# Up projection of a gated MLP: the high weights against both halves of the activations in one product

## The chip, the cores and the metric

The kernel runs on one core of a Trainium2 chip. The time is that of one execution on the device, in microseconds; of several executions the median is given. TensorE (PE) multiplies, with its weight loads (PEld) shown apart; VectorE (DVE), ScalarE (ACT) and GpSimd (POOL) do the elementwise work; SyncE (SP) issues the transfers from device memory. PSUM is the memory that TensorE writes its sums to. A bank of it holds 512 columns of 32-bit numbers on 128 partitions.

## The reference, cut to what matters

One decoder layer over 256 tokens with 2048 channels: a token mixer and then a channel mixer, both normalised and modulated by a vector. The change is in the channel mixer:

```python
def conv_ffn(h, w_up, conv_w, conv_b, w_down):
    a, g = jnp.split(h @ w_up, 2, axis=-1)
    a = causal_dwconv(a, conv_w, conv_b)
    return (jax.nn.silu(a) * g) @ w_down
```

Here `h` is 256 x 2048, `w_up` 2048 x 11264 (5632 columns for `a`, 5632 for the gate `g`), the convolution runs over 3 tokens, and `w_down` is 5632 x 2048. All of it is in 32-bit floats.

## The kernel before, in words

**Three products for one.** TensorE multiplies in a rounded 32-bit format (`F32R`). To keep the accuracy, each operand is split into a high part, rounded to that format, and a low part, the rest: `w = wh + wl`, `x = xh + xl`. The product is taken as `wh xh + wh xl + wl xh`; the last term, low times low, is left out. `load_split` (lines 141 to 168) does this for weights: a transfer of a chunk of 128 x 1024 into `w` (line 124, a ring of seven buffers), a cast on ScalarE into `wh` (line 147) and a subtraction on VectorE into `wl` (line 150). `wh` and `wl` have four buffers each (`WB = (7, 4, 4)`, line 42). The activations are split once, when they are made: `h2T` holds, for each of 16 row blocks k, the high half `h2T[:, k, 0]` and the low half `h2T[:, k, 1]`, 256 tokens each, side by side.

**The up projection.** `up(j)` (lines 1533 to 1566) makes one block j of 128 columns of `a` and the 128 columns of the gate that belong to it; there are 44 blocks. It takes one bank, `ps_up`: the first 256 columns for `a`, the other 256 for the gate. The weights of a side (b = 0 for `a`, 1 for the gate) come in two chunks (hf) of eight row blocks each. For each row block `mm_b` issues three products with the weights as the stationary operand (128 x 128) and the 256 tokens as the moving one. The moving operand is read through `turns`, which alternates between token b and token 128 + b, so the columns of the bank are in that order as well. Blocks 0 and 1 are done otherwise: their product was made before, row-wise, together with the second normalisation, and `up` only transposes it.

After the products `up` does the rest of the block on ScalarE and VectorE: the convolution (an activation with scale and bias at line 1554, four multiply-adds at lines 1558 and 1560), silu (line 1562), the multiplication by the gate (line 1563), and the split of the result into `uTt`, high (line 1565) and low (line 1566). These read `a` and `gate`, two halves of the bank, straight from PSUM.

**The order of the work.** `up` runs for j = 2, 0, 1, 3 ... 21, then the down projection of this half (`proj_rows`, 512 columns to a product, `ps_d`), then `up` for j = 22 ... 43, then the down projection of the second half. In the first half a `Ticker` also feeds in the modulation of the last residual: at `tk.tick(UR)` after each chunk, with `UR = 0.5`, every second chunk brings one transfer of `w_ada` and one multiply-and-sum over 128 x 1024 on VectorE (line 263). The order on each engine in these stretches is made by a planner, which simulates the engines; each engine then works its list off in order and waits by semaphores. Loads are issued on SP's queue in the order of their chunks, as soon as a buffer of the ring is free. Only the second normalisation before and the last normalisation after have their order written out by hand.

**Buffers.** The pool `psm` has four banks, taken in turn by `ps_up`, `ps_d` and others. Small tiles (`t2`) share eight buffers, taken in turn as well; `av`, the working tile of a block, is one of them.

Of the kernel before, what the change touches and what calls it, by code (L numbers as in the profile page):

```python
# [14 lines left out]
P = 128  # L15
S = 256
# [64 lines left out]
def build(ctx: ExitStack, tc: tile.TileContext, d, out, dbg=None):  # L81
    nc = tc.nc
# [8 lines left out]
    psm = ctx.enter_context(tc.tile_pool(name="psm", bufs=4, space=PSUM))  # L91
# [10 lines left out]
    xt = p0.tile([P, 2, D], F32, name="xt", tag="t16")  # L102
# [5 lines left out]
    def mm(o, lhsT, rhs, start, stop):  # L108
        nc.tensor.matmul(o, lhsT, rhs, start=start, stop=stop)  # L109

    def turns(ap):

        return ap.rearrange("p (a b) -> p b a", a=2)

    def t2(shape, name, dt=F32):
        return p0.tile(shape, dt, name=name, tag="t2", bufs=NT2)

    def bank(pool, name, dt=F32):
        return pool.tile([P, 512], dt, name=name, tag="b")
# [21 lines left out]
    def load_split(src, off=0, t=None, after=None, n0=None):  # L141

        n = src.shape[-1]
        if t is None:
            t = load(src)
        wh, wl = halves(off)
        hi = nc.scalar.copy(wh[:, :n], t[:, :n])  # L147
        while moved:
            behind(moved.pop(0)(), hi)
        lows.append(nc.vector.tensor_sub(wl[:, :n], t[:, :n], wh[:, :n]))  # L150
        if after:
            behind(lows[-1], after)
        while added and n0 not in AHEAD[7]:
            behind(lows[-1], added.pop())
        pairs[n0] = hi, lows[-1]
        while slow:
            behind(slow.pop(), lows[-1])
        for nth, ns in AHEAD.items():
            if n0 in ns and nth in wides:
                behind(wides[nth], lows[-1])  # L160
        if n0 == AHEADMOD and blocks:
            behind(blocks[0], hi)
        if fresh:
            fresh[1] -= 1
            if fresh[1] < 0:
                behind(hi, fresh[0])
                fresh.clear()
        return wh, wl
# [5 lines left out]
    def mm_b(ps, wh, wl, i, xt, k, start, stop):  # L174
        a, b = wh[:, i * P:(i + 1) * P], wl[:, i * P:(i + 1) * P]
        xh, xl = [turns(xt[:, k, x, :]) for x in range(2)]
        mm(ps, a, xh, start, False)
        mm(ps, a, xl, False, False)
        mm(ps, b, xh, False, stop)

    def mm_a(ps, xt, k, t, wh, wl, start, stop):
        xh, xl = xt[:, k, 0, t * P:(t + 1) * P], xt[:, k, 1, t * P:(t + 1) * P]
        wh, wl = turns(wh), turns(wl)
        mm(ps, xh, wh, start, False)
        mm(ps, xh, wl, False, False)
        mm(ps, xl, wh, False, stop)
# [33 lines left out]
    for i in range(4):  # L220
        ps = bank(psm, "ps_c")
# [132 lines left out]
    def big(name, offset=0):  # L354

        t = p0.tile([P, 2 * KD * S + OFFN], F32R, name=name, tag="hT")[:, offset:offset + 2 * KD * S]
        return t.rearrange("p (k a b) -> p k a b", k=KD, a=2)
# [111 lines left out]
    with tc.manual_schedule(engines={mybir.EngineType.DVE, mybir.EngineType.Activation, mybir.EngineType.PE}):  # L469
# [5 lines left out]
        sums = [next(second) for _ in range(2)]  # L475
# [290 lines left out]
    for gi, kn in enumerate(GROUPS):  # L766
# [24 lines left out]
        for b, ks in order_b(gi):  # L791
# [3 lines left out]
            ps = psb[j]  # L795
            whole = j < HELD
            shared = j < HELD + 4
            for k in ks:
                need(k0 + k)
                wh, wl = next(wb)  # L800
                o = ps[:, (b % 2) * S:(b % 2 + 1) * S]
                opening = k == 0 and (not shared or b % 2 == 0 and (not whole or gi == 0))
                new = first.setdefault(k, tiles[0]) == tiles[0]
                if tiles[0] <= 5:
                    continue
                end = k == kn - 1 and (not shared or b % 2 == 1 and not (whole and nxt))
                if not new:
                    catch_up()
                    mm_b(o, wh, wl, 0, hT, k0 + k, opening, end)
                else:  # L810
                    mm(o, wh, turns(hT[:, k0 + k, 0, :]), opening, False)
                    mm(o, wl, turns(hT[:, k0 + k, 0, :]), False, False)
                    lag.append((o, wh, turns(hT[:, k0 + k, 1, :]), False, end))
# [19 lines left out]
        for c in range(6):  # L833
            pss = [bank(psm, "ps_a%d" % t) for t in range(2)]
            aw = AW if c < 4 else 512
            for k in range(k0, k0 + kn):
                need(k)
                wh, wl = next(wa if c < 4 else wv)
# [484 lines left out]
    h2T = big("h2T")  # L1323
# [209 lines left out]
    def up(j):  # L1533

        if j < 2:
            ps = bank(psm, "ps_up")
            for t in range(2):
                for b in range(2):
                    c = (2 * b + j) * P
                    nc.tensor.transpose(ps[:, b * S:(b + 1) * S].rearrange("p (k t) -> p t k", t=2)[:, t],  # L1540
                                        ub[t][:, c:c + P], ident)
        else:
            ps = bank(psm, "ps_up")
            for b in range(2):
                for hf in range(2):
                    wh, wl = load_split(d["w_up"][j * 4 + b * 2 + hf], OFFB[hf])
                    for k in range(8):
                        mm_b(ps[:, b * S:(b + 1) * S], wh, wl, k, h2T, hf * 8 + k, hf == 0 and k == 0,
                             hf == 1 and k == 7)
                    tk.tick(UR)  # L1550
        a, gate = ps[:, :S], ps[:, S:]
        fw = lambda i: ffn[:, 3 * j + i:3 * j + i + 1]
        av = t2([P, S], "av")
        nc.scalar.activation(av, a, AF.Identity, bias=ffn[:, R_FB + j:R_FB + j + 1], scale=fw(2))
        aa, vv = [x.rearrange("p (k t) -> p t k", t=2) for x in (a, av)]
        for i in (1, 0):
            sh = 2 - i
            nc.vector.scalar_tensor_tensor(av[:, 2 * sh:], a[:, :S - 2 * sh], fw(i), av[:, 2 * sh:],
                                           op0=ALU.mult, op1=ALU.add)
            nc.vector.scalar_tensor_tensor(vv[:, 1, :sh], aa[:, 0, P - sh:], fw(i), vv[:, 1, :sh],  # L1560
                                           op0=ALU.mult, op1=ALU.add)
        nc.scalar.activation(av, av, AF.Silu)
        nc.vector.tensor_mul(av, av, gate)
        hi, lo = [uTt[:, j % KH, x, :].rearrange("p (t k) -> p t k", t=2) for x in range(2)]
        nc.scalar.copy(hi, vv)
        nc.vector.tensor_sub(lo, vv, hi)
# [4 lines left out]
    for j in (2, 0, 1, *range(3, KH)):  # L1571
        up(j)
        if j == 2:
            for c in range(2):
                tk.add(ada_rows(5, g2, c))
# [3 lines left out]
    for j in range(KH, KF):  # L1579
        up(j)  # L1580
# [189 lines left out]
```

## Time and profile before

| | |
|---|---|
| median of 3 runs | 1386.07 us (1385.78 to 1386.64) |
| the profiled execution | 1386.17 us, its span 1384.2 us |
| TensorE busy | 1364.6 us, 9234 products |
| VectorE busy | 1059.6 us |
| ScalarE busy | 705.6 us |
| granted TensorE clock | 1.0 |
| first half of the up projection | 690 to 908 us of the span |
| first down projection | 909 to 1023 us |
| second half of the up projection | 1023 to 1259 us |
| second down projection and the last normalisation | 1259 to 1384 us |

A row of a group of instructions names line, engine, operation, output <- inputs, shapes, count; then the busy time in us and the mean ns of one; then the idle time of the engine just before them and what ended it. Products overlap in the engine, so the mean duration of one is longer than the time from start to start. Most products have line 109, the helper `mm`, and are told apart by their output tile. In the chain of waits a row gives start, length and what was at work; in a view by stretches, the busy time of each engine in that stretch.

### The profile page before, as it was taken

What the parts mean: (1) busy time and instruction counts of PE and PEld (TensorE: products, weight loads), DVE (VectorE), ACT (ScalarE), POOL (GpSimd) and SP (SyncE); (2) the same over time, 40 slices, a digit from 0 to 9 for tenths busy, and PEclk for the clock granted to TensorE, in tenths of its full rate; (3) what the DMA queues carried; (4) which work ended last, traced back from release to release, by engine and by line L of the source; (5) the groups of instructions that cost most, each with busy time, mean ns of one, the idle gap of its engine ahead of it and who ended that gap; (6) DMA issues with size and microseconds to landing.
All of it is one profiled execution on the core that took longest, in us unless ns stands there. A gap on an engine that the chain in (4) does not pass through costs nothing.

```text
span 1384.2 us, 23506 instructions
## 1 busy us (share of the span) xinstructions
PE 1364.6 (99%) x9234; PEld 1252.2 (90%) x9234; DVE 1059.6 (77%) x1559; ACT 705.6 (51%) x969; POOL 3.6 (0%) x11
## 2 busy tenths in 40 slices
PE   7999999999999999999999999999999999999998
PEld 6999998888778888889699999998899999999887
DVE  8899977888787897789888778755556666665568
ACT  6654455656576444445765554544445445444442
POOL 0000000000000000000000000000000000000000
PEclk9999999999999999999999999999999999999999
DMA  9999978996977999996488878866666666667662
GB/s 375 418 419 375 400 257 283 344 305 237 312 268 288 371 332 369 356 339 226 150 314 298 281 255 292 283 195 204 201 202 198 197 196 197 198 198 199 202 201 84
DMA packets 103310, 374.24 MB, mean 270 GB/s; under 512 B 11168, under 2 KB 11680, under 8 KB 102432
## 3 DMA queue, kind: packets, MB, share of 16 engines
q1 hardware_dynamic: 103200, 372.75, 78.5%
q8 instruction: 72, 1.18, 0.3%
q14 instruction: 38, 0.31, 0.1%
HBM read 370.61 MB, written 2.10 MB: 269 GB/s over the span
## 4 chain that ended last, share of the span: by engine, by line
PE 84%; DVE 7%; DMA 5%; issue 2%; ACT 1%; SPq 0%; DVEq 0%; ACTq 0%
PE ps_up L109 33%; PE ps_d L109 14%; PE ps_mg L109 12%; PE ps_br L109 6%; PE ps_a L109 6%; PE ps_b L109 5%; PE ps_o L109 3%; DVE wl L150 2%; DMA w<-in_w_in_b_dram 2%; PE ps_u L109 2%; DMA w<-in_w_in_a_dram 1%; PE ps_s L109 1%; PE ps_y L109 1%; DMA adaA<-in_w_ada_dram 1%; DMA w<-in_w_o_dram 1%
## 5 line engine op out<-in xcount | busy, mean ns | idle before, releaser
L150 DVE TENSOR_TENSOR wl<-w,wh 128x1024 fp32r<-128x1024 f32 (+1 forms) x470 | 564.4, 1206 | 286.9 <-ACT wh L147 285.7
L147 ACT CAST wh<-w 128x1024 fp32r<-128x1024 f32 (+1 forms) x470 | 484.8, 1036 | 556.1 <-PE ps_up L109 172.8
L109 PE MATMUL ps_up<-h2T,wh 128*128 128x256 f32 x2688 | 450.7, 275 | 0.0
L109 PEld LDWEIGHTS ps_up<-h2T,wh 128*128 128x128 f32 x2688 | 408.7, 192 | 0.1
L109 PE MATMUL ps_up<-h2T,wl 128*128 128x256 f32 x1344 | 369.7, 275 | 0.0
L109 PEld LDWEIGHTS ps_up<-h2T,wl 128*128 128x128 f32 x1344 | 258.0, 192 | 0.0
L109 PE MATMUL ps_d<-wh,uTt 128*128 128x512 f32 (+1 forms) x704 | 198.5, 366 | 0.0
L109 PE MATMUL ps_mg<-wh,hT 128*128 128x512 f32 x512 | 163.1, 389 | 0.0
L263 DVE SCALAR_TENSOR_TENSOR w<-w,crow 128x1024 f32<-128x1024 f32 x132 | 160.8, 1219 | 0.0
L109 PEld LDWEIGHTS ps_d<-wh,uTt 128*128 128x128 f32 x704 | 129.9, 189 | 16.4
L109 PE MATMUL ps_d<-wl,uTt 128*128 128x512 f32 (+1 forms) x352 | 128.8, 366 | 0.0
L109 PE MATMUL ps_b<-hT,wh 128*128 128x256 f32 x768 | 124.9, 277 | 3.8 <-ACT hT L423 2.8
L109 PEld LDWEIGHTS ps_b<-hT,wh 128*128 128x128 f32 x768 | 110.9, 192 | 7.7 <-ACT hT L423 3.5
L109 PEld LDWEIGHTS ps_mg<-wh,hT 128*128 128x128 f32 x512 | 96.8, 189 | 16.0 <-issue 3.1
L109 PE MATMUL ps_a<-wh,hT 128*128 128x392 f32 (+1 forms) x384 | 103.6, 348 | 0.6 <-ACT wh L147 0.6
L109 PE MATMUL ps_mg<-wl,hT 128*128 128x512 f32 x256 | 97.2, 380 | 0.0
L109 PE MATMUL ps_b<-hT,wl 128*128 128x256 f32 x384 | 90.7, 275 | 0.0
L109 PEld LDWEIGHTS ps_a<-wh,hT 128*128 128x128 f32 x384 | 69.4, 189 | 6.2 <-issue 2.2
L109 PEld LDWEIGHTS ps_d<-wl,uTt 128*128 128x128 f32 x352 | 66.7, 189 | 8.4
L109 PE MATMUL ps_a<-wl,hT 128*128 128x392 f32 (+1 forms) x192 | 67.0, 350 | 1.3 <-DVE wl L150 1.2
L109 PEld LDWEIGHTS ps_b<-hT,wl 128*128 128x128 f32 x384 | 67.5, 192 | 0.1
L109 PE MATMUL ps_o<-wh,mgT 128*128 128x512 f32 x192 | 57.3, 379 | 0.0
(317 smaller groups left out, 1341.0 us busy)
## 6 DMA issues: line engine op xcount, KB each, us to landing
w<-in_w_up_dram SPq DMA_DIRECT2D x176, 512.0 KB, 4.4
w<-in_w_ada_dram SPq DMA_DIRECT2D x132, 512.0 KB, 5.1
w<-in_w_down_dram SPq DMA_DIRECT2D x89, 512.0 KB, 4.2
w<-in_w_mg_dram SPq DMA_DIRECT2D x64, 512.0 KB, 5.1
w<-in_w_in_b_dram SPq DMA_DIRECT2D x48, 512.0 KB, 10.6
w<-in_w_br_dram SPq DMA_DIRECT2D x32, 512.0 KB, 5.5
w<-in_w_o_dram SPq DMA_DIRECT2D x32, 512.0 KB, 5.3
adaA<-in_w_ada_dram SPq DMA_DIRECT2D x15, 1024.0 KB, 11.0
```

Source lines behind the costliest of these rows:

```text
L109: nc.tensor.matmul(o, lhsT, rhs, start=start, stop=stop)
L147: hi = nc.scalar.copy(wh[:, :n], t[:, :n])
L150: lows.append(nc.vector.tensor_sub(wl[:, :n], t[:, :n], wh[:, :n]))
L263: ins = nc.vector.scalar_tensor_tensor(t, t, 1.0, crow[:, i * 1024:(i + 1) * 1024], op0=ALU.mult, op1=ALU.mult, accum_out=parts[:, row(m), ...
```

## The change

`mm_c` takes the place of `mm_b` in `up`. It issues two products for a row block: `wh` against high and low halves of `x` together, 512 columns over a whole bank, and `wl` against the high half, 256 columns, accumulated into the bank's second half. So the first half of the bank collects `wh xh`, and the second `wh xl + wl xh`. A bank now holds one side of a block, and a block takes two banks. After each side the second half is copied by ScalarE into a small tile `us`, and VectorE adds the first half to it. The rest of `up` reads these two tiles where it read the two halves of the bank. Blocks 0 and 1 keep their bank. `mm_b` stays for the input projection.

```diff
+    def mm_c(ps, wh, wl, i, xt, k, start, stop):
+        a, b = wh[:, i * P:(i + 1) * P], wl[:, i * P:(i + 1) * P]
+        x = xt[:, k].rearrange("p x (a b) -> p x b a", a=2)
+        mm(ps, a, x, start, False)
+        mm(ps[:, S:], b, x[:, 0], False, stop)
...
         if j < 2:
             ps = bank(psm, "ps_up")
+            a, gate = ps[:, :S], ps[:, S:]
...
         else:
-            ps = bank(psm, "ps_up")
+            sums = []
             for b in range(2):
+                ps = bank(psm, "ps_up")
                 for hf in range(2):
                     wh, wl = load_split(d["w_up"][j * 4 + b * 2 + hf], OFFB[hf])
                     for k in range(8):
-                        mm_b(ps[:, b * S:(b + 1) * S], wh, wl, k, h2T, hf * 8 + k, hf == 0 and k == 0,
-                             hf == 1 and k == 7)
+                        mm_c(ps, wh, wl, k, h2T, hf * 8 + k, hf == 0 and k == 0, hf == 1 and k == 7)
                     tk.tick(UR)
-        a, gate = ps[:, :S], ps[:, S:]
+                whole = t2([P, S], "us")
+                nc.scalar.copy(whole, ps[:, S:])
+                nc.vector.tensor_add(whole, ps[:, :S], whole)
+                sums.append(whole)
+            a, gate = sums
```

## The prediction

> **What bounds the kernel now.** I read the page's busy shares first, then the chain that ended last, then the same chain in order of time over the two halves of the up projection, and last the busy times of each engine in those stretches.
>
> ```profile
> span 1384.2 us, 23506 instructions
> PE 1364.6 (99%) x9234; PEld 1252.2 (90%) x9234; DVE 1059.6 (77%) x1559; ACT 705.6 (51%) x969; POOL 3.6 (0%) x11
> ...
> PE ps_up L109 33%; PE ps_d L109 14%; PE ps_mg L109 12%; PE ps_br L109 6%; PE ps_a L109 6%; PE ps_b L109 5%; PE ps_o L109 3%; DVE wl L150 2%; DMA w<-in_w_in_b_dram 2%; PE ps_u L109 2%; DMA w<-in_w_in_a_dram 1%; PE ps_s L109 1%; PE ps_y L109 1%; DMA adaA<-in_w_ada_dram 1%; DMA w<-in_w_o_dram 1%
> ...
> L109 PE MATMUL ps_up<-h2T,wh 128*128 128x256 f32 x2688 | 450.7, 275 | 0.0
> L109 PE MATMUL ps_up<-h2T,wl 128*128 128x256 f32 x1344 | 369.7, 275 | 0.0
> ```
>
> A third of the span is the products into ps_up, and TensorE stood idle for 0.0 us in front of them. There are 2688 + 1344 = 4032: 42 column blocks (j = 2 to 43) x 2 sides (a, gate) x 16 row blocks x 3. So there are 1344 triples. Their mean of 275 ns is latency, not pace. The pace comes from the chain in order of time (start, length, what):
>
> ```profile
> 682.68 7.43 PE ps_u L109 x32
> ...
> 692.61 10.50 PE ps_up L109 x94
> 703.54 101.84 PE ps_up L109 x912
> ...
> 806.26 101.84 PE ps_up L109 x912
> ...
> 908.97 113.96 PE ps_d L109 x528
> 1022.93 235.84 PE ps_up L109 x2112
> 1258.77 75.13 PE ps_d L109 x348
> ```
>
> 235.84 us / 2112 = 111.67 ns for each product of 256 columns; 101.84 / 912 gives the same. 113.96 / 528 = 215.83 ns for each product of 512 columns in the down projection, whose moving operand is interleaved in the same way. So today a triple takes 3 x 111.67 = 335.0 ns, and one side of a block (16 triples) 5.36 us.
>
> **Why 256 columns cost more than half of 512.** What columns alone cost is read from products of 392 columns in the input projection: a run of them whose first and 57th start stand in the first and last row here, 56 steps apart (timeline of TensorE: start, length):
>
> ```profile
> 135.49 0.33 PE L109 MATMUL ps_a<-wh,hT 128*128 128x392 f32 x1
> ...
> 144.78 0.76 PE L109 MATMUL ps_a<-wh,hT 128*128 128x392 f32 x3
> ```
>
> 9.29 / 56 = 165.9 ns. From 392 to 512 that is 49.9 ns for 120 columns, 0.416 ns each. So 256 columns should take 215.83 - 256 x 0.416 = 109.3 ns, and take 111.67. A rare place in the output projection has one product of 256 columns alone among products of 512, and elsewhere four products of only 32 columns follow each other (timeline of TensorE: start, length; the second row merges three):
>
> ```profile
> 628.23 0.81 PE L109 MATMUL ps_o<-wh,mgT 128*128 128x512 f32 x3
> 628.87 0.27 PE L109 MATMUL ps_o<-gw,mgT 128*128 128x256 f32 x1
> 628.98 0.38 PE L109 MATMUL ps_o<-wl,mgT 128*128 128x512 f32 x1
> 629.20 0.38 PE L109 MATMUL ps_o<-wh,mgT 128*128 128x512 f32 x1
> ```
>
> ```profile
> 247.63 0.61 PE L109 MATMUL ps_kc<-gT,w2t 128*128 128x32 f32 x4
> ...
> L109 PE MATMUL ps_kc<-gT,w2t 128*128 128x32 f32 x4 | 0.6, 276 | 0.0
> ```
>
> Four products of 32 columns are spaced (0.61 - 0.276) / 3 = 0.11 us, the same as 256 columns: about 111.7 ns is what one change of stationary weights takes, and a product shorter than that waits for it. In the other fence the product of 256 follows 0.11 us of start to start, and the next 512 takes 0.22, so 512 and 256 together occupy 0.33 us (629.20 - 628.87). That is the pair that the change makes.
>
> **The change, part by part.**
>
> 1. *TensorE.* Each triple becomes a pair: wh against both halves of h2T as one product of 512 columns, then wl against the high half alone, 256 columns into the bank's second half. One product and one weight load go, the columns streamed stay 768. I take 215.83 for the first. The second hides the load for the next 512 only for its own length, so it pays the load, 111.67. The pair: 327.5 ns against 335.0, 7.5 ns less. Sum: 1344 x 7.5 = 10.08 us. Bounds: below, the 256 could cost its columns alone, 109.3, pair 325.1, 13.3 us off. Above, the new moving operand is a pattern of three levels (half, row, pair), which no row shows. Its nearest rows are the interleaved 512 at 215.83 and the flat 512 of ps_u, 7.43 us / 32 = 232.2. With the latter the pair takes 343.9 and the sum turns into +11.9 us. I take 215.83, since inside each half the order of reading is the one that ps_up and ps_d have now, and only one jump in 512 columns is new. Half a bank as a second target needs no new wait: the same columns are accumulated three times in a row today.
>
> The Trainium skill, "TensorE: Matmul & The Clock Gate", section "Back-to-back issue gap", gives N / 2.4 + 2.5 ns for an isolated product: 215.8 for 512, which this trace has, and 109.2 for 256, which it does not have in a run of them (111.67). By that formula the pair would take 325.0 ns, an estimate that takes 13.4 us off the kernel: the first rival below.
>
> 2. *ScalarE, a new copy* of 256 columns out of PSUM per side, 84 in all. *VectorE, a new addition* per side, 84 in all. The nearest rows, and the instructions whose operand moves from PSUM to SBUF:
>
> ```profile
> L1037 ACT COPY num<-ps_n 128x256 f32<-128x256 f32 x8 | 2.7, 391 | 0.6 <-PE ps_n L109 0.5
> L1554 ACT ACTIVATE av<-ps_up,ffn 128x256 f32<-128x256 f32 x44 | 24.3, 557 | 0.0
> L574 ACT ACTIVATE cvt<-accM,prm 128x256 f32<-128x256 f32 x8 | 4.4, 594 | 1.0 <-DVE accM L823 1.0
> ...
> L1563 DVE TENSOR_TENSOR av<-av,ps_up 128x256 f32<-128x256 f32 x44 | 18.1, 415 | 0.5 <-ACT av L1562 0.5
> L1558 DVE SCALAR_TENSOR_TENSOR av<-ps_up,ffn,av 128x254 f32<-128x254 f32 x44 | 20.9, 475 | 0.0
> L578 DVE SCALAR_TENSOR_TENSOR cvt<-accM,prm,cvt 128x254 f32<-128x254 f32 x8 | 3.5, 478 | 0.0
> ```
>
> A column block j gets 2 x 0.391 + (0.594 - 0.557) = 0.82 us of ScalarE and 2 x 0.415 + 2 x 0.003 = 0.84 us of VectorE. Whether that is hidden is read per stretch (busy us of PE, PEld, DVE, ACT, POOL; clock, DMA share, GB/s):
>
> ```profile
> 703.54:805.38 101.84, 101.84 (x915) 101.84 (x914) 83.57 (x143) 55.06 (x75) 0.00 (x0) 1.00 0.83 279
> 806.26:908.10 101.84, 101.84 (x914) 101.84 (x914) 79.59 (x126) 51.58 (x69) 0.00 (x0) 1.00 0.83 278
> ...
> 1022.93:1258.77 235.84, 235.84 (x2114) 235.84 (x2113) 145.72 (x218) 116.91 (x152) 0.00 (x0) 1.00 0.66 197
> ```
>
> A block takes 96 x 111.67 ns = 10.72 us now and 10.48 after. In the first stretch, where VectorE also does the modulation's products, it is busy 83.57 / 101.84 x 10.72 = 8.80 us per block; 9.64 after, 92% of 10.48. ScalarE goes from 5.80 to 6.62, 63%. In the second half VectorE goes from 6.62 to 7.46, 71%. The work is covered by TensorE everywhere, by 0.84 us per block where it is tightest. DMA goes from a share of 0.83 to 0.85 by the shorter block; the clock is 1.00 and stays so. I cost the copies and additions at nothing; were that cover gone, they would cost what exceeds 0.84 us per block.
>
> 3. *The waits.* The copy waits for the last product of its side, and ScalarE's casts queue behind it; the addition waits for the copy, and VectorE's subtractions queue behind it. TensorE waits for both. How much it can stand:
>
> ```profile
> 765.11 1.05 ACT L147 CAST wh<-w 128x1024 fp32r<-128x1024 f32 x1 [1.02 <-PE ps_up L109]
> ...
> 766.19 1.23 DVE L150 TENSOR_TENSOR wl<-w,wh 128x1024 fp32r<-128x1024 f32 x1 [1.11 <-ACT wh L147]
> ```
>
> A cast starts when TensorE gives a buffer back and its split is done 766.19 + 1.23 - 765.11 = 2.3 us later. There are four buffers, so TensorE has three other chunks of 10.48 / 4 = 2.62 us to go, 7.9 us: 5.6 us of cover. One copy ahead of a cast takes 0.39. A VectorE that has fallen behind also finds the copy done, so the wait eats slack rather than adding to a lag. SP's loads follow the subtractions that free the w slots; their order is unchanged.
>
> 4. *Buffers.* A block takes two of the four banks instead of one, but each is free after its addition, not after the multiplication by the gate some 6 us later; the bank wanted next was last taken four sides, some 21 us, back. The three t2 tiles per block instead of one go round eight buffers: a slot is wanted again after 2.7 blocks. Nothing waits.
>
> 5. *The ends.* The last block of each half reaches uTt two ScalarE-VectorE steps (0.8 us) later per side. The down projection reads that block last of 22, in its eleventh chunk; ten chunks of 12 products at 215.83 ns, 26 us, lie before. Its work and the tail after it only start earlier by what TensorE gained.
>
> The sum: 1386.17 (the profiled execution: span 1384.2 and about 2 us around it) - 10.08 = 1376.1. The median of the runs, 1386.07, lies 0.1 lower: 1376.0.
>
> **Rivals.**
>
> *The load hides wholly* (1372.8 us). Pairs at 325.1, as bounded above: 13.3 us off. For it: the 0.33 us of the pair at 628.87 are rounded, and a load that starts early enough behind a 512 would be done. Against: each load so far is one product ahead, and the one for the next 512 has only a 256 to hide behind. 4%.
>
> *The cost goes with each run of 256 columns, not with the weight change* (1386, the change not doing what it says). The 512 would cost 2 x 111.67. Against: 32 columns cost the same 0.11 us. 4%.
>
> *VectorE paces the first half, no more* (1380.5 us). Additions that wait 0.5 us each there keep the 19 blocks of the two first stretches (2 x 912 / 96) at the old 10.72; the other 23 gain 0.24 each, 5.5 us. 4%.
>
> *Slower: VectorE stalls at the additions* (1399.8 us). If at each addition it finds ScalarE in a cast of 1.05 us ahead of the copy, a block costs it 9.64 + 2.1 = 11.7 us, 1.0 over today's pace: 19 blocks lose 19.2 us, 23 gain 5.5. It decides from 0.84 us of stall per block. For it: 92% busy, and queues in order. Against: the stall happens only to a VectorE that is ahead, with the 5.6 us of cover still in hand. 5%.
>
> *Slower: the three-level pattern streams like the flat one*, 1386.1 + 11.9 = 1398.0. For it: flat and interleaved 512s do differ, 232 against 216. Against: the pattern stays interleaved inside. 5%.
>
> **How the numbers follow.** 78% for the sum, with its own range of 1374.5 to 1378, which allows a microsecond or two for another order of work from the planner. A measurement of this kernel tells about 0.2% (2.8 us) from no change. Faster by more: 78 + 4 + 4 = 86%; same: 4%; slower: 10%. The range of 1372 to 1381 holds the sum, the hidden load and the half gain, 86%; the two slower bounds stay outside with 10%.
>
> **What would show it.** Right: two starts in ps_up 327.5 ns apart; the second half's 704 pairs in 230.6 us instead of 235.84; TensorE without idle time in front of ps_up; the down projection at 215.83. Wrong: a ps_up product of 512 spaced over 220 ns (pattern), TensorE idle in front of ps_up released by wl (VectorE), VectorE idle released by the new copy for more than 0.8 us per block, or a longer stretch after 1333.92 (the tail took it back).

## The result, and the profile after

The changed kernel takes 1376.53 us (median of 4 runs, 1375.77 to 1377.45) against 1386.3 us; the ratio is 0.993 (95% interval 0.9913 to 0.9947). That is 9.8 us less, where 10.1 were forecast. The profiled execution took 1377.45 us.

The page of the changed kernel, its busy times and the groups of products into ps_up:

```profile
span 1375.4 us, 20986 instructions
PE 1356.4 (99%) x7890; PEld 1208.5 (88%) x7890; DVE 1089.1 (79%) x1643; ACT 733.5 (53%) x1053; POOL 3.6 (0%) x11
...
L109 PE MATMUL ps_up<-h2T,wh 128*128 128x512 f32 x1344 | 440.6, 382 | 0.0
L109 PE MATMUL ps_up<-h2T,wl 128*128 128x256 f32 x1344 | 366.3, 273 | 0.0
```

1344 products went, one per row block and side, and TensorE still waits 0.0 us in front of those that are left. Its chain in order of time (start, length, what):

```profile
693.83 2.84 PE ps_up L109 x17
...
704.97 99.56 PE ps_up L109 x608
...
805.40 99.56 PE ps_up L109 x608
...
905.84 113.96 PE ps_d L109 x528
1019.80 230.56 PE ps_up L109 x1408
1250.36 75.13 PE ps_d L109 x348
```

230.56 us for 704 pairs are 327.5 ns each, and 99.56 for 304 give the same, against 335.0 for a triple before. The second half of the up projection takes 230.56 us where it took 235.84. The down projection is at 113.96 and 75.13 us as before, so nothing is given back behind. The timeline of TensorE shows the pair itself:

```profile
760.15 0.38 PE L109 MATMUL ps_up<-h2T,wh 128*128 128x512 f32 x1
760.37 0.27 PE L109 MATMUL ps_up<-h2T,wl 128*128 128x256 f32 x1
760.48 0.38 PE L109 MATMUL ps_up<-h2T,wh 128*128 128x512 f32 x1
```

The new work lies on ScalarE and VectorE. First the busy times by stretch (PE, PEld, DVE, ACT, POOL; clock, DMA share, GB/s), then the groups of the new and moved operations within the first half of the up projection:

```profile
704.97:804.53 99.56, 99.56 (x610) 91.50 (x610) 89.76 (x162) 61.03 (x94) 0.00 (x0) 1.00 0.85 285
805.40:904.96 99.56, 99.56 (x611) 91.56 (x610) 86.19 (x145) 57.83 (x88) 0.00 (x0) 1.00 0.85 284
...
1019.80:1250.36 230.56, 230.56 (x1409) 211.96 (x1409) 161.34 (x261) 132.02 (x195) 0.00 (x0) 1.00 0.67 202
```

```profile
L1560 DVE TENSOR_TENSOR us<-ps_up,us 128x256 f32<-128x256 f32 x38 | 15.9, 417 | 0.0
...
L1559 ACT COPY us<-ps_up 128x256 f32<-128x256 f32 x38 | 13.9, 367 | 0.0
L1565 ACT ACTIVATE av<-us,ffn 128x256 f32<-128x256 f32 x19 | 11.4, 602 | 0.0
```

VectorE is busy 89.76 of 99.56 us, 9.45 us per block of 10.48; ScalarE 6.42. No engine waits in front of the copies or the additions.

The three long stretches became 2.28, 2.28 and 5.28 us shorter, 9.84 us together for 1312 of the 1344 pairs. The other 32 lie in the opening. The first product into ps_up, after the change and before it:

```profile
691.78 0.22 PE ps_up L109
```

```profile
690.12 0.22 PE ps_up L109 x2
```

From there to the first long stretch it is 13.19 us now (691.78 to 704.97) and was 13.42 (690.12 to 703.54), 0.23 less. So the pairs gain 10.07 us. In the profiled executions the spans differ by 8.8 us only: the up projection starts 1.66 us later, at the end of work that the change does not touch, and the work behind the second down projection is 0.38 us shorter (49.90 against 50.28).

Nearly all of the later start, 1.54 us, is there early: a run of 120 products into ps_a in the input projection begins at 136.76 us where it began at 135.22. The clock of TensorE was lower at the kernel's beginning. The stretch from 20 to 60 us, of the changed kernel and then of the one before:

```profile
20.00:60.00 40.00, 37.90 (x293) 37.15 (x293) 32.83 (x33) 26.66 (x42) 0.00 (x0) 0.96 1.03 418
```

```profile
20.00:60.00 40.00, 37.26 (x293) 36.00 (x293) 33.65 (x36) 26.31 (x42) 0.00 (x0) 1.00 1.03 418
```

In the first 20 us it was 0.91 against 1.00. That the clock is the cause is not shown: the run with five more VectorE operations, below, had the full clock through the first 60 us, and its run into ps_a begins at 136.71. What moves this start stays open. The runs of this kernel lie up to 1.7 us apart, so differences of that size are read from the stretches here, not from the medians.

### The profile page after: what moved, and what is told of

Same layout as the page of the kernel before. It is cut to its first block, busy times and chain, and to the rows that moved or that the text cites. A ratio compares the mean times of both kernels' runs of the same rounds, so it can differ in the third digit from the quotient of the medians.

```text
span 1375.4 us, 20986 instructions
## 1 busy us (share of the span) xinstructions
PE 1356.4 (99%) x7890; PEld 1208.5 (88%) x7890; DVE 1089.1 (79%) x1643; ACT 733.5 (53%) x1053; POOL 3.6 (0%) x11
## 4 chain that ended last, share of the span: by engine, by line
PE 85%; DVE 8%; DMA 2%; issue 2%; ACT 2%; SPq 0%; DVEq 0%; ACTq 0%
PE ps_up L109 32%; PE ps_d L109 14%; PE ps_mg L109 12%; PE ps_b L109 7%; PE ps_br L109 6%; PE ps_a L109 5%; PE ps_o L109 3%; DVE wl L150 3%; PE ps_u L109 2%; DVE adaA L251 1%; DMA w<-in_w_in_b_dram 1%; PE ps_s L109 1%; PE ps_y L109 1%; DVE adaB L251 1%; PE ps_hid L109 1%
## 5 line engine op out<-in xcount | busy, mean ns | idle before, releaser
L109 PE MATMUL ps_up<-h2T,wh 128*128 128x512 f32 x1344 | 440.6, 382 | 0.0
L109 PEld LDWEIGHTS ps_up<-h2T,wh 128*128 128x128 f32 x1344 | 253.9, 189 | 35.4
```

## The experiments

My theory: a product of 256 columns is shorter than the load of the next weights, so a triple pays three loads of 111.67 ns and a pair pays 215.83 + 111.67; copies, additions and waits are covered. The rivals are those of the prediction. That a triple pays three loads, though two of its products have the same weights, is seen in the rows of the weight loads, before and after: there is one load for each product, and the loads of wh are half as many after the change, with 35.4 us of idle time in front of them.

```profile
L109 PEld LDWEIGHTS ps_up<-h2T,wh 128*128 128x128 f32 x2688 | 408.7, 192 | 0.1
```

```profile
L109 PEld LDWEIGHTS ps_up<-h2T,wh 128*128 128x128 f32 x1344 | 253.9, 189 | 35.4
```

**The product of 512 as two of 256 again**, all else left as changed.

```diff
-        mm(ps, a, x, start, False)
+        mm(ps[:, :S], a, x[:, 0], start, False)
+        mm(ps[:, S:], a, x[:, 1], False, False)
         mm(ps[:, S:], b, x[:, 0], False, stop)
```

> Everything of the change stays (a bank per side, the copy, the addition), but the product of 512 columns is issued as two of 256 again, high half into the first half of the bank, low half into the second. My theory (the whole gain is the weight load that a product of 256 columns cannot hide, 7.5 ns per triple): the spacing returns to 111.67 ns per product, 335.0 per triple, and the time returns to that of the kernel before, 1386.3, 10.1 above the changed kernel, with copies and additions hidden. Rival (part of the gain is from the bank that comes free earlier, or copies and additions cost something that the gain covers): 1380 or less in the first case, 1388 or more in the second.

Measured: 1386.86 us, ratio to the kernel before 1.0002 (0.9993 to 1.0012). The chain in order of time:

```profile
706.29 101.84 PE ps_up L109 x912
...
1025.68 235.84 PE ps_up L109 x2112
```

These are the lengths of the kernel before to the hundredth. So the gain is in the one merged product; the other buffers, copies and additions together leave the lengths as they were.

**The product of the low weights on 128 columns.**

```diff
-        mm(ps[:, S:], b, x[:, 0], False, stop)
+        mm(ps[:, S:S + P], b, x[:, 0, :P // 2], False, stop)
```

> The changed kernel, with the product of the low weights on 128 of the 256 columns only (the low weights' term is left out for the other half of the tokens). My theory (a product shorter than the load of the next weights takes the load, 111.67 ns): the pair stays at 327.5 ns and the time at 1376.5, although a sixth of all columns is gone. Rival (time goes with columns plus a fixed part per product): 128 columns x 0.4167 ns less per pair, 53 ns x 1344 = 72 us less, 1305.

Measured: 1376.21 us, ratio 0.9926 (0.9909 to 0.9943), the time of the changed kernel. The chain, and the timeline of TensorE and of its weight loads:

```profile
1018.24 230.50 PE ps_up L109 x1408
```

```profile
1020.64 0.43 PE L109 MATMUL ps_up<-h2T,wh 128*128 128x512 f32 x1
1020.92 0.22 PE L109 MATMUL ps_up<-h2T,wl 128*128 128x128 f32 x1
1020.97 0.43 PE L109 MATMUL ps_up<-h2T,wh 128*128 128x512 f32 x1
```

```profile
1020.92 0.19 PEld L109 LDWEIGHTS ps_up<-h2T,wh 128*128 128x128 f32 x1
1021.03 0.19 PEld L109 LDWEIGHTS ps_up<-h2T,wl 128*128 128x128 f32 x1
```

A sixth of all columns left out saves 0.06 us of 230.56. The pair is 327.4 ns whether its second product has 256 columns or 128. The record shows where the time goes. A 512 starts 0.05 us behind the product of 128 (1020.92 to 1020.97), but the product behind a 512 starts only 0.28 us after it (1020.64 to 1020.92), not 0.22. The load for the 512 starts together with the product of 128, at 1020.92, and the next load 0.11 us later, at 1021.03. Counted from there, 0.216 us for the 512 end at 1021.25, and the next product of 128 starts at 1021.24. So the 512 is recorded early and waits for its weights. The profile does not show this as a wait; it is read from the starts, and no run here multiplies without a new load.

The two rivals about the product of 256 fall as well: with the load wholly hidden a pair would take 325.1 ns, and if each run of 256 columns had its price, the merged product would have won nothing. A time that goes with the columns, 1305 us here, falls with this run.

**The product of 512 reads the tokens flat.**

```diff
-        mm(ps, a, x, start, False)
+        mm(ps, a, xt[:, k].rearrange("p x t -> p (x t)"), start, False)
```

> The changed kernel, with the product of 512 columns reading the two halves of the activations flat, in natural order of tokens, and not alternating between token b and token 128 + b (the first term is so summed into columns of other tokens). My theory (alternation is what keeps 512 columns at 215.8 ns, as ps_d has, while the flat ps_u takes 232): the pair goes to about 343.9 ns and the time up by 22 us, 1398. Rival (reading order does not matter here, ps_u is slower for another reason): 1376.5.

Measured: 1398.24 us, ratio 1.0085 (1.007 to 1.01), slower than the kernel before. The chain:

```profile
1029.20 241.68 PE ps_up L109 x1408
```

343.3 ns for a pair, so 231.6 for a flat 512 against 215.8 alternating: near the 232.2 that the rows of ps_u gave. The order in which tokens are read is worth 21.7 us here, twice the gain of the change, and the three-level pattern keeps the faster one. Why flat reading is slower, no run here shows.

**Without the copy and the addition.**

```diff
-                whole = t2([P, S], "us")
-                nc.scalar.copy(whole, ps[:, S:])
-                nc.vector.tensor_add(whole, ps[:, :S], whole)
-                sums.append(whole)
+                sums.append(ps[:, :S])
```

> The changed kernel without the copy and the addition (the mixed terms, high weights times low activations and low weights times high activations, are left out of what the rest of the block reads; they are still multiplied). My theory (both are covered by TensorE, 84 copies and 84 additions cost nothing): 1376.5 within 1 us. Rival (they cost something in the first half, where VectorE is busy 90%): 1374 or less.

Measured: 1377.67 us, ratio 0.9937 (0.9922 to 0.9952), 1.1 us above the changed kernel and so just outside the microsecond that I allowed. Its chain:

```profile
705.84 99.56 PE ps_up L109 x608
...
1020.67 230.56 PE ps_up L109 x1408
```

The stretches have the same lengths as with the join. The difference lies ahead of them, since in the profiled execution the first starts 0.9 us later (705.84 against 704.97); the clock from 665 to 670 us was 0.66 there, and 1.00 in the changed kernel's profile. The join costs TensorE nothing.

**How much VectorE can take: one, three and five more operations per side.** Each adds this loop, with n = 1, 3, 5:

```diff
                 nc.vector.tensor_add(whole, ps[:, :S], whole)
+                for _ in range(n):
+                    nc.vector.scalar_tensor_tensor(whole, whole, 1.0, whole, op0=ALU.mult, op1=ALU.max)
                 sums.append(whole)
```

> The changed kernel with one more VectorE operation of 256 columns behind each addition (it writes the same values back). My theory (VectorE has 10.48 - 9.45 = 1.03 us per block to spare in the first half, by the changed kernel's profile): two more operations of 0.39 us per block make 10.23 of 10.48 us, still covered: 1376.5 to 1378. Rival (the cover is already gone through waits in VectorE's list): 0.78 us x 19 blocks, 1391.

Measured: 1377.55 us, ratio 0.993 (0.9914 to 0.9947), with stretches of 99.56, 99.56 and 230.56 us as without them. As expected, it is covered: VectorE is busy 187.41 us of the first half's 200.87, where the changed kernel had 176.82.

> The changed kernel with three more VectorE operations of 256 columns behind each addition (they write the same values back). My theory: six more operations of 0.39 us per block make 11.8 us in the first half, 1.3 over TensorE's 10.48, so VectorE sets the pace there and 19 blocks lose some 25 us: 1401 (1395 to 1410); the second half (7.33 + 2.34 = 9.7 us) stays covered. Rival (TensorE's buffers carry it, or VectorE's share of busy time hides waits that can be filled): under 1385.

Measured: 1382.7 us, ratio 0.9971 (0.9961 to 0.9982). That is 6.2 us lost, not 25: outside the range that I gave and under 1385, where the rival stood. Busy times by stage, the first half of the up projection and the down projection behind it, first of the changed kernel and then of this one; then the one wait of TensorE in this kernel's timeline, and the two stretches around and behind it:

```profile
704.97:905.84 200.87, 200.87 (x1233) 184.81 (x1233) 176.82 (x308) 120.61 (x181) 0.00 (x0) 1.00 0.84 283
905.84:1019.80 113.96, 113.96 (x529) 99.79 (x529) 63.25 (x64) 47.66 (x50) 0.00 (x0) 1.00 0.66 202
```

```profile
704.29:909.97 205.68, 202.89 (x1234) 186.16 (x1233) 205.68 (x410) 116.51 (x177) 0.00 (x0) 0.99 0.82 275
909.97:1023.93 113.96, 113.96 (x529) 99.83 (x529) 68.63 (x81) 50.00 (x54) 0.00 (x0) 1.00 0.67 206
```

```profile
780.56 0.45 PE L109 MATMUL ps_up<-h2T,wh 128*128 128x512 f32 x1 [2.79 <-DVE us L1560]
```

```profile
780.00:784.00 4.00, 3.44 (x12) 2.98 (x13) 4.00 (x11) 0.64 (x2) 0.00 (x0) 0.64 0.91 309
784.00:790.00 6.00, 6.00 (x37) 5.48 (x36) 6.00 (x16) 3.75 (x7) 0.00 (x0) 0.96 0.23 77
```

VectorE works without a break through the whole first half, and TensorE runs on except for one wait of 2.79 us, ended by the addition that frees a bank. The forecast had three terms wrong:

- The spare time. I took 1.03 us per block from the first stretch alone, 19.6 us for 19 blocks. Over both stretches the changed kernel leaves VectorE 200.87 - 176.82 = 24.05 us.
- The price. I took 0.39 us for an operation, 44.5 us for 114. They added 34.3 us of busy time in the two stages together (205.68 + 68.63 - 176.82 - 63.25), 0.30 each.
- The delay. I let none of the work be put off. In the down projection VectorE is busy 68.63 us where the changed kernel had 63.25, so 5.4 us were put off and cost nothing.

34.3 - 24.05 - 5.4 leaves 4.8 us, and in this execution the first half is 4.8 us longer. It is the fastest of the seven (1381.74 us); the slowest took 1384.83.

> The changed kernel with five more VectorE operations of 256 columns behind each addition (they write the same values back). In the run with three more, VectorE was busy all the time in the first half and 6.2 us were lost, not 25. Theory now (VectorE may fall behind by some 14 us, as far as the four banks reach, about three sides of 5.24 us; this backlog is worked off in the down projection behind, and only what exceeds it is lost): ten more operations of 0.34 us make 12.85 us per block, 2.37 over TensorE's 10.48, times 19 is 45 us, less 14: 31 us lost, and a few more in the second half (7.33 + 3.4 = 10.7 us): 1400 to 1414. Rival (the extra operations always find idle time, however many): under 1392.

Measured: 1409.36 us, ratio 1.0155 (1.0139 to 1.017): 32.8 us lost where the theory of a backlog said 31. What TensorE waited for in the whole up projection (us in total, times, longest), and the busy times of the first half, the down projection behind it, the second half and the last down projection:

```profile
PE ps_up L109 <- DVE us L1560: 21.7, 10, 4.2
```

```profile
704.40:937.68 233.28, 211.55 (x1234) 191.32 (x1233) 229.25 (x477) 118.04 (x178) 0.00 (x0) 0.96 0.73 243
937.68:1051.65 113.97, 113.97 (x530) 99.80 (x529) 72.52 (x94) 49.99 (x53) 0.00 (x0) 1.00 0.67 204
1051.65:1282.20 230.55, 230.55 (x1409) 212.06 (x1409) 227.03 (x472) 133.94 (x195) 0.00 (x0) 1.00 0.65 201
1282.20:1357.30 75.10, 75.10 (x350) 65.76 (x349) 48.08 (x63) 32.07 (x33) 0.00 (x0) 1.00 0.66 203
```

The number came out, but its terms did not; that it is so near is in part luck. The 190 extra operations of the first half added 61.7 us (229.25 + 72.52 - 176.82 - 63.25), and 24.05 of that fitted into VectorE's spare time. Put off into the down projection were 9.3 us (72.52 against 63.25), not 14. VectorE itself stood idle for 4.0 of the 233.28 us. 61.7 - 24.05 - 9.3 + 4.0 gives 32.4 us, by which the first half is longer in this execution (233.28 against 200.87).

The second half loses nothing, but not because a backlog takes up an excess: there is none. Its work was forecast at 10.7 us per block, and it just fits: VectorE is busy 227.03 of 230.55 us, and 3.3 us more than in the changed kernel (48.08 against 44.74) follow in the last down projection.

So part of VectorE's arrears costs nothing: 5.4 us in one run and 9.3 in the other, at the end of the first half. How far it may fall behind is not shown. All ten waits of TensorE end with the addition, which frees a bank, and a bank is wanted again after three more sides of 5.24 us. That fits a limit by the banks, but no run had another number of them, and the order of VectorE's list, which the planner makes anew for each kernel, may have a part.

**Filler in TensorE's idle time before the second normalisation**, where some runs showed the half clock.

```diff
-        wait(2)
+        wait(9)
```

> The changed kernel with nine filler products of TensorE in place of two in its idle time of 1.7 us before the second normalisation (they write a bank that nothing reads). Several runs show 3.4 us at half the clock right behind that idle time, and the up projection begins about 1 us later in them. Theory (the idle time makes the clock drop; filled, it does not): no half-clock window near 666 us, median 0.5 to 1.5 us below the changed kernel's, 1375.5. Rival (the filler delays the work behind it, or the drop comes for another reason): 1376.5 or more.

Measured: 1376.73 us, ratio 0.9929 (0.9916 to 0.9941), the changed kernel's time. The 0.5 to 1.5 us that I expected were not won. The profiled run had the full clock there, but so had the changed kernel's own without the filler, so this run cannot tell whether the filler helps. What decides about the half clock at that place stays open.

No run here is clearly faster than the changed kernel.

## Why the prediction was right

*What a pair costs.* 327.5 ns were worked out and 327.5 measured, from rows of other parts of the kernel: 215.83 from ps_d, 111.67 from ps_up, and their neighbourhood from a single place in ps_o. The reason given, the load of the next weights, holds: half the columns of the short product changed nothing. The formula that the Trainium skill gives for an isolated product ("TensorE: Matmul & The Clock Gate", section "Back-to-back issue gap"), by which I estimated 325.0 for the pair, does not fit here; its 109.2 ns for 256 columns leaves the load out, and the trace decides.

*The pattern with three levels.* It streams like the interleaved one, as taken. The price put on the flat one was right too: 1398.24 measured, 1398.0 worked out.

*Copy and addition.* 0.391 us for a copy and 0.415 for an addition were taken from neighbours, and 0.367 and 0.417 measured. In the first stretch VectorE came to 9.45 us per block in place of 9.64, because an operation starts before the one ahead of it has ended, and each adds less than its length. They are covered, as stated; removing them shortened no stretch.

*The waits.* TensorE waits for neither. But the statement that they would cost "what exceeds 0.84 us per block" was too strict, and with it the limit in the rival in which VectorE stalls (1399.8). Over the whole first half the changed kernel leaves VectorE 24.05 us for 19 blocks, 1.27 per block, since the second stretch has less work than the first; and of what goes beyond, 5.4 us in one run and 9.3 in another cost nothing. I had counted the four buffers of split weights (5.6 us) as the reserve. In the two runs in which VectorE fell behind, TensorE never waited for a split, only for additions, so it was the block's other work that came late.

*The ends.* The down projections kept their lengths, 113.96 and 75.13 us. The sum was 10.08 us, and the stretches show 10.07 of it: 9.84 in the three long ones and 0.23 in the opening. The medians show 9.8.

## What to carry to other kernels

Read a product's price from start to start, over many of them, and compare different widths: where 256, 128 and 32 columns cost the same, as here, the load of the stationary operand is being paid, and two products that share a stationary operand should be one, as wide as the bank allows. Additions and copies that this needs are free as long as the other engines keep up over the whole stage; take their spare time from the whole stage too, not from its tightest stretch. When a moving operand is rearranged, keep the order in which it is read fastest: flat reading would have cost twice what the merging won.

## What was not expected

VectorE at 100% for 205 us cost only some 5 us, since the extra work found more spare time than I had counted and part of it slid into the next stage. And a wait of TensorE of 2.79 us was followed by some 3.4 us at half the clock: a mean of 0.64 over 4 us is 2.9 us at a half, and 0.96 over the next 6 us another 0.5; in steps of half a microsecond the view shows 0.50 from 781.5 to 784.5 us. So that wait cost more than its own length. In the run with five more operations the clock was 0.96 over the first half, and TensorE was busy 211.55 us with what takes 200.87 at full clock; its waits, 21.7 us, are only two thirds of what was lost.
